# An mLSTM and sparse-attention trunk: nine low parts of weights by ScalarE and an accumulating transfer, with a later low product and other buffer counts

## The chip, the cores and the metric

One core of a Trainium2 chip. The engines are PE (TensorE, matmuls), DVE (VectorE), ACT (ScalarE), POOL (GpSimd) and SP (SyncE, which issues most transfers); 16 DMA engines move data. The metric is the device time of one execution in microseconds (us); lower is better. Before the change the median of 3 runs is 383.62 us (383.25 to 387.83).

## The reference

A decoder trunk of two layers on x of 256 tokens by 1024 channels, in float32. Layer 0 is an mLSTM mixer, layer 1 native sparse attention; each normalises, multiplies by an input weight matrix, mixes, gates, multiplies by an output matrix and adds to x. Cut to the parts that the change touches:

```
x_in, z = jnp.split(h @ w_in, 2, axis=-1)              # h: normalised x; w_in: 1024 x 4096
conv = sum(x_pad[:, tap:tap + S] * conv_w[tap] for tap in range(4))
x_conv = silu(conv + conv_b)
q, k = headwise(x_conv, w_q), headwise(x_conv, w_k)    # 4x4 blocks on the diagonal
v = headwise(x_in, w_v)
gates = concat([q, k, v]) @ w_if + b_if
hh = mlstm_chunkwise(q, k, v, gates)                   # 4 heads of 512
x = x + ((norm(hh) * ln_w + skip * x_conv) * silu(z)) @ w_out
# layer 1: q, compressed / selected / window keys and values, z, gates = rmsnorm(x) @ w_in ...
```

## The kernel before

All large weights are streamed from HBM in 44 units of 1 MB (value units are smaller), in the order of a list `plan`: units 0 to 7 give x_in (two per head), 8 to 15 z, 16 to 23 the output matrix of layer 0, the rest layer 1 (keys and queries, values, z, output). `next_unit` uses unit i and calls `ahead`, so that units up to i+2 have been loaded (`LOOK = 2`).

`load_unit` (L261 to L277) loads a unit in two halves. For each half SP issues a load into a raw buffer `wr` (4 buffers, `WR`), ACT copies it into `wh`, rounded to the matmul format fp32r (L274), and the low part `wl` = raw - wh is a subtraction on POOL if the pair (unit, half) is in the list `ON_POOL`, on DVE otherwise (L275). `wh` and `wl` have 4 buffers each (`WH`). `ON_POOL` holds the second halves (number 1) of units 3 to 10 and 12 to 23, of every other unit from 24 on, and three first halves.

The activations are split in the same way into hh and hl. `project_channels` (L399) multiplies one unit: for 8 slices k and 2 column blocks c three matmuls of 128 columns by 256 tokens each, wh by hh (i = 0), wh by hl (i = 1) and wl by hh (i = 2), 48 in all, at L406. Slices 0 to 3 come from the first half. `LAG` delays the products i = 1 and i = 2 by so many steps of k; unit 1 has its own entry in `LAGS`. `out_project` (L689) and `project_tokens` (L769 to L771) use the other units.

In the first stage, head by head, DVE evacuates x_in with the row scale rb (L433, `xin`; rb is copied at L384, and half of it is made at L385, `rb1h`). `blockdiag` (L390, the multiply at L393) builds on POOL the block-diagonal matrices `m` from a buffer set of 7 (`M2`), two for each of 4 heads. DVE forms products of gate weights (L458, `wtmp`) and sums them into m and q (L459). The convolution is started by ACT (L471, L475) and, in head 0, added up on POOL (L477); DVE adds the other taps (L482), ACT applies silu (L484). PE then makes v from xin and m (L499), q from xc and m (L492, copied by ACT at L493), and the scores from q and xc (L506, L507).

In layer 1 h (L987) is transposed to h1T (L991) and used by PE at L994; `kb` (L811) are keys, half of them written by POOL; L860 are 14 gating multiplications on POOL whose results PE reads at L892.

A scheduler reorders the code: it places every instruction in its engine's queue by a simulated timeline, so that the order on an engine is not that of the code, and a change of one duration or buffer count can move others. Each engine then works through its queue in order.

Of the kernel before, what the change touches and what calls it, by code (L numbers as in the profile page):

```python
# [11 lines left out]
AF = mybir.ActivationFunctionType  # L12
OP = mybir.AluOpType
# [10 lines left out]
G = 4  # L24
NEG = -1e30
F4 = 8
M2 = 7
VA = 2
V_POOL = (0, 2)
SC = 7  # L30
YM = (1,)
LOOK = 2
PSB = {"ps": 2, "pt": 2, "px": 2, "acc0": 1, "acc1": 1}
WH = 4
WR = 4
PB = 5
PV = 4
# [4 lines left out]
VB = 0  # L42
NSW = 1

LAG = (0, 0)
LAGS = {1: (0, 1)}

TR = ((0, 0),)
# [19 lines left out]
NOT_POOL = (0, 1, 2, 11)  # L68
BOTH = (15, 16, 17)
ON_POOL = [(i, 1) for i in list(range(24)) + list(range(24, 48, 2)) if i not in NOT_POOL] + [(i, 0) for i in BOTH]  # L70


_C = {}
# [129 lines left out]
def trunk(ctx, tc, a, out, dbg=None):  # L203
    nc = tc.nc
# [13 lines left out]
    def T(*x, **k):  # L218
        return tile_of(pool[0], *x, **k)

    def TS(*x, **k):
        return tile_of(sb, *x, **k)

    def PS(shape=(P, 512), tag="ps", name="ps"):
        uid[0] += 1
        return pp.tile(list(shape), F32, tag=tag, bufs=PSB[tag], name=f"{name}_{uid[0]}")

    f32 = lambda t: t.bitcast(F32)
    V, A, GP, PE = nc.vector, nc.scalar, nc.gpsimd, nc.tensor
# [11 lines left out]
    def load_x(i):  # L241

        k = slice(2 * i % 4, 2 * i % 4 + 2)
        nc.sync.dma_start(xch0[i // 2][:, k, :].rearrange("p k s -> p (k s)"), a["xt"][:, i * 2 * S:(i + 1) * 2 * S])
# [13 lines left out]
    def load_unit(src, row, nk, nn):  # L258

        hk = nk // 2  # L260
        halves = []  # L261
        for i in range(2):
            raw = TS([P, hk, nn], tag="wr", bufs=WR)
            hi = TS([P, hk, nn], F32R, tag="wh", bufs=WH)
            lo = TS([P, hk, nn], F32R, tag="wl", bufs=WH)
            parts = 1 if loaded else 2
            for j in range(parts):
                if not loaded:
                    load_x(2 * i + j)
                w = hk // parts  # L270
                k = slice(j * w, (j + 1) * w)
                o = i * hk + j * w
                nc.sync.dma_start(raw[:, k, :].rearrange("p k n -> p (k n)"), src[row * P:(row + 1) * P, o * nn:(o + w) * nn])
                A.activation(hi[:, k, :], raw[:, k, :], AF.Copy)  # L274
                (GP if (len(loaded), i) in ON_POOL else V).tensor_tensor(lo[:, k, :], raw[:, k, :], f32(hi[:, k, :]), op=OP.subtract)  # L275
            halves.append((hi, lo))
        return halves  # L277

# [8 lines left out]
    loaded = []  # L287
    used = [0]

    def ahead(n):  # L290
        while len(loaded) < min(n, len(plan)):
            loaded.append(load_unit(*plan[len(loaded)]))
# [98 lines left out]
    def blockdiag(src, dt, n=P):  # L391
        t = T([P, 4, n], dt, tag="m2", bufs=M2)
        GP.tensor_tensor(t[:, :, 0:P].rearrange("p c (n j) -> p c n j", j=4),  # L393
                         src[:, :, None, :].to_broadcast([P, 4, 32, 4]), bm, op=OP.mult)
        return t

    def project_channels(src, row, evac, tag="px"):

        halves = next_unit(src, row, 256)  # L399
        ps = PS((P, 2, S), tag=tag)  # L400
        lags = LAGS.get(used[0] - 1, LAG)

# [23 lines left out]
    for h in range(NH):  # L426
# [61 lines left out]
        for c2 in range(2):  # L488
            ps = PS((P, 2, S))
            for c in range(2):  # L490
                k = 2 * c2 + c
# [88 lines left out]

    oh_ = T([64, 4, P], tag="m2", bufs=M2, name="oh_")
    nc.scalar.dma_start(oh_.rearrange("p h m -> p (h m)"), a["cst"][0:64, n_res:])
    oh = T([64, 4, P], F32R, tag="m2", bufs=M2, name="oh")
    GP.tensor_copy(oh, oh_)
    hns = []
    for h in range(NH):
# [17 lines left out]
        for tb in range(2):  # L604
# [3 lines left out]
            for t in three:  # L608
                jb, o, i, j = t
# [31 lines left out]
    for h in range(NH):  # L641
# [8 lines left out]
        for c2 in range(2):  # L650
# [5 lines left out]
            for c in range(2):  # L656
                k = 2 * c2 + c
# [481 lines left out]
```

## Time and profile before

| | before |
|---|---|
| median of 3 runs | 383.62 us (383.25 to 387.83) |
| profiled execution | 386.84 us, span 385.1 us, mean granted clock 0.959 |
| PE busy | 359.1 us (93%), 2399 instructions |
| DVE busy | 284.8 us (74%), 535 |
| ACT busy | 212.8 us (55%), 405 |
| POOL busy | 192.9 us (50%), 165 |
| chain that ended last | PE 68%, DVE 21%, issue 4%, POOL 3% |
| moved by DMA | 52.74 MB, mean 137 GB/s |

Times within the span count from its start. An engine's busy share over the whole span mixes stages, so the stages are read one by one. A view by waits names, for an idle engine, what ended its idle time; where two engines slow each other there is no wait, and only durations of equal instructions tell it. The granted clock is the share of TensorE's full speed, 2.4 GHz, that was granted; 0.5 is the lower level, 1.2 GHz.

### The profile page before, as it was taken

The numbers are of one execution on the slowest core, as the hardware profiler recorded it, in microseconds if no ns is written. First come the engines' busy times: TensorE is split into PE (matmuls) and PEld (weight loads), VectorE is DVE, ScalarE is ACT, GpSimd is POOL, SyncE is SP. The second block draws the span as 40 slices with busy tenths as digits, with TensorE's granted clock in tenths as the row PEclk, the third lists the DMA queues.
The fourth block names the chain that finished last, engine by engine and source line by source line (L and its number), as shares of the span: only waits on it lengthen the run. The fifth ranks groups of instructions, "written<-read, shape, count | busy, mean of one in ns | idle before, by whom it ended". The sixth has DMA issues, their size and how long they took to land.

```text
span 385.1 us, 6551 instructions
## 1 busy us (share of the span) xinstructions
PE 359.1 (93%) x2399; PEld 319.4 (83%) x2399; DVE 284.8 (74%) x535; ACT 212.8 (55%) x405; POOL 192.9 (50%) x165
## 2 busy tenths in 40 slices
PE   6998797999999999999999999979799989999992
PEld 6997796999999989778888899969799777777761
DVE  5987998678587799996346476799879966685415
ACT  6626284665667564536554542522779648777414
POOL 5238934483324455956345231557434956346303
PEclk9699698999999999999999999989989989999997
DMA  7768323323334311437465962305376331200002
GB/s 260 287 214 299 134 73 108 110 78 143 134 131 154 132 69 45 131 99 252 171 235 199 357 215 75 97 26 155 112 262 217 112 111 55 83 29 2 0 2 109
DMA packets 16880, 52.74 MB, mean 137 GB/s; under 512 B 2000, under 2 KB 2384, under 8 KB 16848
## 3 DMA queue, kind: packets, MB, share of 16 engines
q1 hardware_dynamic: 15472, 48.71, 37.0%
q10 hardware_dynamic: 1376, 3.61, 2.7%
q8 instruction: 19, 0.31, 0.3%
q14 instruction: 13, 0.11, 0.1%
HBM read 50.87 MB, written 1.05 MB: 135 GB/s over the span
## 4 chain that ended last, share of the span: by engine, by line
PE 68%; DVE 21%; issue 4%; POOL 3%; ACT 1%; DMA 1%; POOLq 0%; DVEq 0%
PE ps L406 27%; PE ps L689 16%; DVE xc L482 3%; DVE wl L275 2%; PE ps L506 2%; DVE wtmp L458 2%; PE ps L904 2%; PE ps L892 2%; PE ps L979 2%; PE ps L770 2%; PE ps L769 2%; PE ps L771 2%; DVE r L664 2%; DVE xc L660 1%; PE ps L908 1%
## 5 line engine op out<-in xcount | busy, mean ns | idle before, releaser
L406 PE MATMUL ps<-hT,wh 128*128 128x256 f32 x832 | 163.2, 293 | 0.8 <-ACT wh L274 0.8
L406 PEld LDWEIGHTS ps<-hT,wh 128*128 128x128 f32 x832 | 135.7, 198 | 2.7 <-ACT wh L274 1.1
L275 POOL TENSOR_TENSOR wl<-wr,wh 128x1024 fp32r<-128x1024 f32 (+1 forms) x33 | 85.4, 2593 | 84.9 <-ACT wh L274 72.7
L274 ACT ACTIVATE wh<-wr 128x1024 fp32r<-128x1024 f32 (+2 forms) x90 | 89.3, 1000 | 67.5 <-PE ps L406 27.9
L406 PE MATMUL ps<-hT,wl 128*128 128x256 f32 x416 | 122.1, 294 | 3.5 <-POOL wl L275 1.8
L275 DVE TENSOR_TENSOR wl<-wr,wh 128x1024 fp32r<-128x1024 f32 (+2 forms) x57 | 75.0, 1320 | 29.0 <-ACT wh L274 28.9
L406 PEld LDWEIGHTS ps<-hT,wl 128*128 128x128 f32 x416 | 82.2, 198 | 5.6 <-DVE wl L275 2.2
L689 PE MATMUL ps<-wh,r 128*128 128x512 f32 x128 | 40.9, 399 | 0.5 <-DVE r L664 0.5
L482 DVE SCALAR_TENSOR_TENSOR xc<-xin,pka,xc 128x256 f32<-128x256 f32 x44 | 30.3, 745 | 2.1 <-ACT xc L471 2.1
L689 PEld LDWEIGHTS ps<-wh,r 128*128 128x128 f32 x128 | 23.9, 188 | 6.8 <-DVE r L664 1.4
L689 PE MATMUL ps<-wl,r 128*128 128x512 f32 x64 | 25.0, 396 | 0.0
L689 PE MATMUL ps<-wh,y 128*128 128x512 f32 x64 | 21.9, 405 | 0.0
L770 PE MATMUL ps<-wl,hT 128*128 128x280 f32 (+1 forms) x48 | 16.3, 342 | 1.9 <-DVE wl L275 1.9
L771 PE MATMUL ps<-wh,hT 128*128 128x280 f32 (+1 forms) x48 | 15.8, 339 | 0.0
L769 PE MATMUL ps<-wh,hT 128*128 128x280 f32 (+1 forms) x48 | 15.8, 344 | 0.0
L499 PE MATMUL ps<-m,xin 128*128 128x136 f32 x64 | 10.6, 321 | 5.1 <-DVE m L459 4.4
L798 POOL TENSOR_TENSOR swap<-swap,trig 128x512 f32<-128x512 f32 x6 | 11.0, 1832 | 8.5 <-DMA swap<-kraw 8.5
L689 PEld LDWEIGHTS ps<-wh,y 128*128 128x128 f32 x64 | 11.9, 189 | 3.2 <-issue 0.8
L689 PEld LDWEIGHTS ps<-wl,r 128*128 128x128 f32 x64 | 12.0, 188 | 2.8
L471 ACT ACTIVATE xc<-xin,pka 128x256 f32<-128x256 f32 x16 | 8.9, 592 | 9.8 <-DVE xin L433 9.8
L499 PEld LDWEIGHTS ps<-m,xin 128*128 128x128 f32 x64 | 9.7, 226 | 5.4 <-POOL m L393 5.4
L506 PE MATMUL ps<-q,xc 128*128 128x264 f32 x32 | 11.0, 429 | 2.6 <-ACT q L493 2.6
(472 smaller groups left out, 698.4 us busy)
## 6 DMA issues: line engine op xcount, KB each, us to landing
wr<-in_wi_dram SPq DMA_DIRECT2D x34, 512.0 KB
wr<-in_wo_dram SPq DMA_DIRECT2D x24, 512.0 KB
wr<-in_wi2k_dram SPq DMA_DIRECT2D x12, 512.0 KB
wr<-in_wi2z_dram SPq DMA_DIRECT2D x8, 512.0 KB
wr<-in_wi2v_dram SPq DMA_DIRECT2D x8, 280.0 KB
cw<-in_cw_dram ACTq DMA_DIRECT2D x4, 512.0 KB
xch<-in_xt_dram SPq DMA_DIRECT2D x4, 256.0 KB
wr<-in_wi_dram SPq DMA_DIRECT2D x4, 256.0 KB
```

The source lines that it names most:

```text
L274: A.activation(hi[:, k, :], raw[:, k, :], AF.Copy)
L275: (GP if (len(loaded), i) in ON_POOL else V).tensor_tensor(lo[:, k, :], raw[:, k, :], f32(hi[:, k, :]), op=OP.subtract)
L406: PE.matmul(ps[:, c, :], w, (hl if i == 1 else hh)[:, k, :], start=(k, c, i) == (0, 0, 0), stop=(k, i) == (KT - 1, 2), skip_group_check=True)
L471: A.activation(xc[:, c, :], xin[:, c, 0:S], AF.Identity, scale=tap_w(0, c), bias=cbias)
L482: V.scalar_tensor_tensor(xc[:, c, :], xin[:, c, tap:tap + S], tap_w(tap, c), xc[:, c, :], op0=OP.mult, op1=OP.add)
L499: PE.matmul(ps[:, c, :] if c < 3 else rest[:, tb, :], xin[:, c, 3 + tb * P:3 + (tb + 1) * P], bdv[:, c, :], start=True, stop=True)
L506: PE.matmul(ps[:, 0:SG], xc[:, c, 0:P], q[:, c, :], start=c == 0, stop=False, skip_group_check=True)
L689: PE.matmul(acc, l, r[:, k % 2, cols], start=first and i == 0, stop=last and i == 2)
L769: PE.matmul(o_, lh, hi[:, k % 2, :], start=kt == 0, stop=False)
L770: PE.matmul(o_, lh, lo[:, k % 2, :], start=False, stop=False)
L771: PE.matmul(o_, ll, hi[:, k % 2, :], start=False, stop=kt == KT - 1)
L798: (GP, V)[RE[1]].tensor_tensor(sw, sw, turn(1), op=OP.mult)
```

## The change

For pairs of `ON_POOL` up to unit 12, that is the second halves of units 3 to 10 and 12, nine in all, the subtraction on POOL is replaced: ACT writes -raw, rounded as `wh` is, into `wl`, and POOL issues a transfer from `wr` to `wl`, in SBUF, that adds raw into what stands there. The other 24 POOL subtractions stay. The low product comes four steps of k later in every unit but unit 1 (`LAG`), `wh` and `wl` get 5 buffers, `m` gets 5 instead of 7, and the scratch for descriptors of POOL's transfers is made smaller.

```diff
-M2 = 7
+M2 = 5
-WH = 4
+WH = 5
-LAG = (0, 0)
+LAG = (0, 4)
 LAGS = {1: (0, 1)}
 ON_POOL = [(i, 1) for i in list(range(24)) + list(range(24, 48, 2)) if i not in NOT_POOL] + [(i, 0) for i in BOTH]
+BY_DMA = [(i, j) for i, j in ON_POOL if i <= 12]
                 A.activation(hi[:, k, :], raw[:, k, :], AF.Copy)
-                (GP if (len(loaded), i) in ON_POOL else V).tensor_tensor(lo[:, k, :], raw[:, k, :], f32(hi[:, k, :]), op=OP.subtract)
+                if (len(loaded), i) in BY_DMA:
+
+                    A.activation(lo[:, k, :], raw[:, k, :], AF.Copy, scale=-1.0)
+                    GP.dma_start(out=lo[:, k, :].rearrange("p k n -> p (k n)"), in_=raw[:, k, :].rearrange("p k n -> p (k n)"), accum_op=OP.add)
+                else:
+                    (GP if (len(loaded), i) in ON_POOL else V).tensor_tensor(lo[:, k, :], raw[:, k, :], f32(hi[:, k, :]), op=OP.subtract)
-    nc = _bacc.Bacc("TRN2", target_bir_lowering=False, num_devices=1)
+    nc = _bacc.Bacc("TRN2", target_bir_lowering=False, num_devices=1, dynamic_dma_scratch_size=4096)
```

The scheduler's order changes with it. Three places matter below. (Line numbers of the changed kernel are higher by 7 from L277 on; numbers after names count tiles and differ by a few.)

POOL at the start of the first stage, before: wl_259, wl_396 and wl_458 are the second halves of units 3, 4 and 5, the m are blockdiagonals, xin_578 the clearing of an edge of head 2's xin.

```order
20 L275 TENSOR_TENSOR wl_259<-wr_257,wh_258 128x1024
21 L477 TENSOR_TENSOR xc_324<-xc_324,x_61_325 128x512
22 L393 TENSOR_TENSOR m_57_317<-AT_315,cst_70 128x512
23 L393 TENSOR_TENSOR m_58_319<-pka_71,cst_70 128x4x128
...
27 L393 TENSOR_TENSOR m_117_706<-pka_71,cst_70 128x4x128
28 L393 TENSOR_TENSOR m_145_896<-AT_315,cst_70 128x512
29 L477 TENSOR_TENSOR xc_324<-xc_324,x_61_325 128x512
30 L275 TENSOR_TENSOR wl_396<-wr_394,wh_395 128x1024
31 L275 TENSOR_TENSOR wl_458<-wr_456,wh_457 128x1024
34 L428 MEMSET xin_578 128x4x3
```

And with the change:

```order
20 L280 DMA wl_259<-wr_257 128x1024
21 L484 TENSOR_TENSOR xc_325<-xc_325,x_61_326 128x512
22 L400 TENSOR_TENSOR m_57_318<-AT_316,cst_70 128x512
23 L400 TENSOR_TENSOR m_58_320<-pka_71,cst_70 128x4x128
...
26 L400 TENSOR_TENSOR m_116_709<-AT_316,cst_70 128x512
27 L484 TENSOR_TENSOR xc_325<-xc_325,x_61_326 128x512
28 L280 DMA wl_397<-wr_395 128x1024
29 L400 TENSOR_TENSOR m_117_711<-pka_71,cst_70 128x4x128
30 L435 MEMSET xin_581 128x4x3
31 L280 DMA wl_460<-wr_458 128x1024
```

Five blockdiagonals instead of seven stand together, the subtractions have become transfers, and the third transfer stands behind m_117 and the memset of xin_581.

DVE in the same stage, from the first convolution steps to the sum that fills head 0's second blockdiagonal (m2_58), before:

```order
33 L482 SCALAR_TENSOR_TENSOR xc_60_324<-xin_33_159,pka_7_71,xc_60_324 128x256 x2
34 L458 TENSOR_TENSOR wtmp_59_321<-wif_47_242,pka_7_71 128x128
35 L458 TENSOR_TENSOR wtmp_63_346<-wif_46_241,pka_7_71 128x256
36 L482 SCALAR_TENSOR_TENSOR xc_60_324<-xin_33_159,pka_7_71,xc_60_324 128x256 x2
37 L459 TENSOR_REDUCE m2_58_319<-wtmp_59_321 128x4x8
38 L459 TENSOR_REDUCE q_62_345<-wtmp_63_346 128x4x8
```

And with the change:

```order
33 L489 SCALAR_TENSOR_TENSOR xc_60_325<-xin_33_159,pka_7_71,xc_60_325 128x256 x4
34 L465 TENSOR_TENSOR wtmp_59_322<-wif_47_242,pka_7_71 128x128
35 L465 TENSOR_TENSOR wtmp_63_347<-wif_46_241,pka_7_71 128x256
36 L466 TENSOR_REDUCE m2_58_320<-wtmp_59_322 128x4x8
37 L466 TENSOR_REDUCE q_62_346<-wtmp_63_347 128x4x8
```

The same seven instructions stand ahead of the sums. On PE, 14 more matmuls (10 of L406, 4 of L499) stand ahead of the first score matmul L506; on DVE in layer 1 kb no longer stands between h (L987) and h1T (L991).

POOL in layer 1, before: wl_3112 is the second half of the third z unit of layer 1, the p are gatings.

```order
100 L798 TENSOR_TENSOR swap_2188<-swap_2188,trig_2186 128x512
101 L860 TENSOR_SCALAR p__486_2821<-p__486_2821,sums_2816,gt_2192 128x128
...
108 L860 TENSOR_SCALAR p__508_2885<-p__508_2885,sums_2853,gt_2192 128x256 x2
109 L275 TENSOR_TENSOR wl_3112<-wr_3110,wh_3111 128x1024
110 L860 TENSOR_SCALAR p__560_3173<-p__560_3173,sums_3168,gt_2192 128x128
```

And with the change:

```order
99 L282 TENSOR_TENSOR wl_2987<-wr_2985,wh_2986 128x1024
100 L282 TENSOR_TENSOR wl_3121<-wr_3119,wh_3120 128x1024
101 L867 TENSOR_SCALAR p__486_2830<-p__486_2830,sums_2825,gt_2201 128x128
102 L867 TENSOR_SCALAR p__489_2839<-p__489_2839,sums_2825,gt_2201 128x256 x2
```

The subtraction has moved from behind the gatings to ahead of them.

## Rows read from the trace of the kernel before

**Rows 1.** Windows: length, busy us (instructions) of PE, PEld, DVE, ACT, POOL; clock, DMA share, GB/s.

```profile
36.00:63.00 27.00, 19.31 (x130) 18.52 (x129) 26.76 (x39) 12.30 (x20) 17.79 (x14) 0.87 0.37 131
86.00:130.00 44.00, 44.00 (x346) 42.52 (x346) 31.85 (x49) 27.63 (x41) 16.99 (x9) 1.00 0.41 144
...
40.00:50.00 10.00, 8.27 (x46) 8.12 (x47) 10.00 (x13) 4.21 (x8) 8.60 (x5) 0.67 0.44 156
```

**Rows 2.** Timeline of PE: start, us, operation, count, idle time before and its releaser.

```profile
41.03 3.97 PE L499 MATMUL ps<-m,xin 128*128 128x136 f32 x16 [4.40 <-DVE m L459]
...
62.66 0.71 PE L506 MATMUL ps<-q,xc 128*128 128x264 f32 x2 [2.60 <-ACT q L493]
...
254.97 0.69 PE L994 MATMUL ps<-h1T,pkb 128*128 128x64 f32 x2 [2.70 <-DVE h1T L991]
...
309.27 0.46 PE L406 MATMUL ps<-hT,wl 128*128 128x256 f32 x1 [1.78 <-POOL wl L275]
```

**Rows 3.** Chain that ended last, in order of time: start, us, what.

```profile
31.09 0.04 DVE wl L275
...
59.76 1.28 DVE xc L482 x3
...
109.34 11.38 PE ps L406 x95
```

**Rows 4.** Timeline of ACT.

```profile
20.64 1.06 ACT L274 ACTIVATE wh<-wr 128x1024 fp32r<-128x1024 f32 x1 [1.88 <-DMA wr<-in_wi_dram]
...
40.16 1.06 ACT L274 ACTIVATE wh<-wr 128x1024 fp32r<-128x1024 f32 x1 [5.42 <-DMA wr<-in_wi_dram]
...
61.06 1.06 ACT L484 ACTIVATE xc<-xc 128x1024 f32<-128x1024 f32 x1 [3.45 <-DVE xc L482]
```

**Rows 5.** Timeline of DVE.

```profile
23.60 0.42 DVE L384 COPY rb<-ps 128x256 f32<-128x256 f32 x1 [1.72 <-PE ps L373]
...
25.08 2.50 DVE L385 TENSOR_SCALAR rb1h<-rb 128x256 f32<-128x256 f32 x1
...
33.54 2.45 DVE L482 SCALAR_TENSOR_TENSOR xc<-xin,pka,xc 128x256 f32<-128x256 f32 x2
35.91 2.31 DVE L458 TENSOR_TENSOR wtmp<-wif,pka 128x128 f32<-128x128 f32 x2
...
42.73 4.96 DVE L458 TENSOR_TENSOR wtmp<-wif,pka 128x128 f32<-128x128 f32 x2
...
49.02 0.61 DVE L458 TENSOR_TENSOR wtmp<-wif,pka 128x128 f32<-128x128 f32 x2
...
50.65 0.87 DVE L482 SCALAR_TENSOR_TENSOR xc<-xin,pka,xc 128x256 f32<-128x256 f32 x2
...
251.31 3.29 DVE L811 TENSOR_TENSOR kb<-rot,ka 64x1024 fp32r<-64x1024 f32 x1
```

**Rows 6.** Timeline of POOL (the first of its seven blockdiagonals, L393, among them).

```profile
24.05 3.37 POOL L275 TENSOR_TENSOR wl<-wr,wh 128x1024 fp32r<-128x1024 f32 x1 [4.96 <-ACT wh L274]
...
31.43 2.04 POOL L393 TENSOR_TENSOR m<-AT,cst 128x512 f32<-128x512 f32 x1
...
41.69 5.72 POOL L275 TENSOR_TENSOR wl<-wr,wh 128x1024 fp32r<-128x1024 f32 x2
...
306.87 2.34 POOL L275 TENSOR_TENSOR wl<-wr,wh 128x1024 fp32r<-128x1024 f32 x1
```

**Rows 7.** Instructions grouped by line and shape: busy us, mean ns, idle time before.

```profile
L275 POOL TENSOR_TENSOR wl<-wr,wh 128x1024 fp32r<-128x1024 f32 x31 | 82.5, 2666 | 74.3 <-ACT wh L274 62.1 <-PE ps L970 9.2 <-issue 1.8
L274 ACT ACTIVATE wh<-wr 128x1024 fp32r<-128x1024 f32 x78 | 81.7, 1054 | 55.3 <-PE ps L406 21.1 <-PE ps L689 14.9 <-DMA wr<-in_wi_dram 8.6
```

**Rows 8.** Timeline of SP's queue: issues of loads, 512 KB each, and their count.

```profile
16.20 9.31 SPq L273 DMA_DIRECT2D wr<-in_wi_dram  x5
...
30.63 0.47 SPq L273 DMA_DIRECT2D wr<-in_wi_dram  x1
```

**Rows 9.** Windows of line L406 alone: length, PE and PEld busy (instructions), clock, DMA share, GB/s.

```profile
63.00:130.00 67.00, 47.36 (x356) 44.18 (x356) 0.97 0.36 126
```

## The prediction

> **What bounds the kernel now.** I read the windows first, to see where TensorE is not full. From 86 to 130 us PE is busy in all 44.00 us; in 36:63 it is busy 19.31 of 27.00 us, while DVE is busy 26.76 of 27.00 and POOL 17.79 [rows 1]. So the one long stretch in which PE starves is 36 to 63 us: 27.00 - 19.31 = 7.69 us idle, and in addition a granted clock of 0.67 in 40:50, where part of the work ran at the lower level, 1.2 GHz [rows 1].
>
> PE's timeline, then, says for whom it waits. In this stretch it stood 4.40 us before 41.03 for DVE's blockdiagonal m and 2.60 us before 62.66 for ACT's q; two later waits are of the same size, 2.70 us for h1T and 1.78 us for a POOL low part [rows 2]. The chain of waits has nothing but DVE and its issue gaps from 31.09 to 61.04 us [rows 3]. In ACT's timeline q comes right behind the silu at 61.06, for which ACT had waited 3.45 us on the convolution, DVE's [rows 4].
>
> Why DVE is so slow there is in the timelines of DVE and POOL side by side. The same pair of wtmp products takes 0.61 us at 49.02, when POOL is idle, 4.96 us at 42.73 and 2.31 us at 35.91 [rows 5]; POOL runs two wl subtractions from 41.69 for 5.72 us, and its seven blockdiagonals from 31.43 on, 1.1 to 2.0 us each, to about 40.3 [rows 6]. Two convolution steps take 0.87 us at 50.65 and 2.45 us at 33.54. The copy rb1h takes 2.50 us at 25.08, inside the wl of 24.05 to 27.42 [rows 5, 6]. So in this stretch DVE bounds PE, and POOL's subtractions and blockdiagonals make DVE slow.
>
> **The change, part by part.**
>
> *Nine POOL subtractions removed.* At 2666 ns each [rows 7] that is 24.0 us of POOL between 24 and 130 us; what counts is what DVE did beside them on the chain. (a) wl_259 beside rb1h: rb1h read one 128x256 tensor, as the copy ahead of it, which took 0.42 us [rows 5]: 2.50 - 0.42 = 2.1 us earlier xin, for which ACT's convolution copies wait. (b) wl_396 and wl_458 beside wtmp: 4.96 - 0.61 = 4.35 us. The other six lie where PE is full [rows 1] and give nothing.
>
> *M2 from 7 to 5.* Two of seven blockdiagonals leave the run of POOL work at 31.43 to 40.3 us and come later, one by one. The excess of DVE there is (2.45 - 0.87) x 2 + (2.31 - 0.61) = 4.86 us, the second pair of convolution steps, at 38.15, having the same 2.45 us; two sevenths of it are 1.4 us. Sum on DVE's chain: 2.1 + 4.35 + 1.4 = 7.85 us.
>
> Not all of this reaches PE. The stretch from 49 to 61 us, convolutions beside no subtraction, keeps its price, and q still stands behind the silu; fourteen more matmuls stand ahead of q's consumers, which fill 14 x 0.12 = 1.7 us of the wait (0.12 us is the spacing where PE is full: 11.38 us for 95 matmuls in the chain [rows 3]). I take 6 us. Upper bound: all idle time, 7.69, with the clock that comes back, about 9 (the clock's 1.3 is an estimate: 0.33 x 10 us in 40:50 less some 2 us in which PE was idle there [rows 1]). Lower bound 1, if new neighbours on DVE (below) take it.
>
> *Nine ACT copies added.* 1054 ns each, as hi [rows 7]: 9.5 us. ACT is busy 12.30 of 27.00 in 36:63 and has idle time before its copies [rows 1, 4]: 0. Without that cover three of them, ahead of 45 us, would cost 3.2 us.
>
> *Nine accumulating transfers added.* No row shows one. Nearest rows: a plain load of the same 512 KB, issued at 16.20 and read at 20.64, so 20.64 - 16.20 = 4.4 us; one behind about 2 MB of other loads, issued at 30.63 and read at 40.16, 9.5 us [rows 4, 8]. From below, nothing excludes 2.67, the POOL subtraction itself [rows 7]. I take 5 us, near the first, since the DMA engines are busy 0.37 of 36:63 [rows 1]. By the Trainium skill ("DMA: Bandwidth & Descriptors", "Anatomy of one DMA — SWDGE (gpsimd) path") a transfer issued by GpSimd takes about 2.0 us plus its bytes at 436 GB/s, an estimate of 3.2 us here, and the term below would be 0; no run so far shows it.
>
> *LAG (0,4)* pays for that: the second half's low part is now needed eight matmuls before a unit's end, 40 instead of 26 matmuls into it, 40 x 0.12 = 4.8 us after its start; hi of the second half is needed at 16 instead of 24, 1 us earlier, covered by a lookahead of two units. The tight place is wl_460: on POOL its transfer stands behind blockdiagonal m_117 (which needs a buffer PE frees) and behind the xin memset, that is behind DVE's last convolution of head 0, which I put at about 45 us; landing 50, needed by PE at about 50. Price 1 us, bounds 0 and 9.5 - 4.4 = 5.1, rounded to 6 with the clock.
>
> *WH 4 to 5* costs nothing in time; the descriptor scratch neither.
>
> *Later places, only moved.* (c) DVE at 251.31 spends 3.29 us on kb, ahead of h1T, for which PE waits 2.70 us [rows 2, 5, 6]; now kb is no longer between h and h1T. Take 2; bounds 4.2 (with the lower clock after it) and -1, if the new order makes another wait. (d) POOL's wl at 306.87, behind fourteen gatings, held PE for 1.78 us until 309.27 [rows 2, 6]; now that wl is taken ahead of the gatings. Take 2 with the clock; bounds 3.9 and -2, as the gatings move by 2.34 us and PE's L892 uses them.
>
> **Sum.** 6 + 2 + 2 - 1 = 9 us. Against the profiled execution: 386.84 - 9 = 377.8. That execution lies 3.2 us above the median of 383.62, so on the median 374.6 (2.3% less).
>
> **Rivals.**
>
> *The gain is absorbed.* For it: DVE was busy 26.76 of 27.00 us; the blockdiagonals that remain still run beside the convolutions, and two come later, beside others; ACT waits 3.45 us for the silu's input whatever POOL does. Then only 1 to 4 us of (a) and (b) reach PE, (c) and (d) cancel with new waits: 380 to 384. Against it: 4.35 us of DVE's chain goes at one place that PE demonstrably waited for.
>
> *Slower: transfers land so late that raw buffers run out.* A raw buffer was free once the subtraction had read it; now it is held until the transfer has landed. There are four, two units' worth. In 63:130 PE does 356 weight matmuls, 7.4 units in 67 us, 9.0 us a unit [rows 9], so a buffer may be held 18.1 us: load 4.4, hi 1.05, negated copy 1.05, landing L. It breaks even at L = 11.6 us. Beyond that each two units lose L - 11.6; at 15 us that is 3.4 x 3.7 = 12.6 us, 377.8 + 12.6 - 3.2 = 387.2; slower by over 2% (391.3) from L = 16. For it: DMA 9.5 us under load [rows 4, 8], and nothing shows what an add costs the DMA engines. Against: a share of 0.41 in 86:130 leaves them more than half idle [rows 1].
>
> *Transfers wait for DVE.* POOL and DVE hold each other up in rows 5 and 6; if preparing a transfer does so too, in 36:63 (DVE busy 99%) each waits for a gap. With one group of 2.5 us for each of wl_397 and wl_460, PE waits up to 5 us, the sum is 4, 379.6 on the median; in 86:130 DVE has 12 us free of 44 [rows 1] and nothing is lost. The Trainium skill states such a rule ("SBUF — State Buffer", "SBUF: two separate sides"): GpSimd cannot write descriptors while VectorE holds the port pair they share, and the transfer only seems slow. The mutual slowing in rows 5 and 6 agrees with a shared port; no run yet shows a transfer.
>
> *The change doesn't do what it says*: hardly possible, the order lists nine transfers in place of nine subtractions.
>
> **How the numbers follow.** Forecast (366 to 379) 0.58; absorbed 0.18; waiting for DVE 0.12; landings of 16 us or more, with any stall at a place not foreseen that costs as much, 0.12. The predicted time is 374.6. The range 366 to 388 reaches down to the largest sum of bounds (9 + 4.2 + 3.9 = 17.1 us of gain, 366.5) and up to landings of 15 us (387.2); it leaves out the last case. A measurement can tell about 2% here: below 375.9 is faster, above 391.3 slower. Of the forecast 0.45 lies below 375.9, since there is more room below the sum than above it; its other 0.13 and the first two rivals lie within 2%; the last case is slower.
>
> **What would show it.** Right: wtmp pairs at about 0.6 us and rb1h at 0.4; PE's wait for m under 1.5 us and for q smaller; PE busy above 24 of 27 us in the stretch; waits for h1T and for POOL's wl gone; no wait for a transfer's wl above 1 us. Wrong: PE or SP waiting for transfers, landings above 10 us, DVE steps still 1.2 us each, or L499 and L506 waits of the old size with another releaser.

## The result: 1.5% slower

The changed kernel takes 389.79 us (median of 4 runs, 389.31 to 391.61) against 384.38 us for the kernel before beside it (383.25 to 387.83): a ratio of 1.0149, 95% interval 1.0103 to 1.0196. The forecast was 374.6 us; the time lies above the range of 366 to 388, on the other side of no change. The profiled execution has a span of 387.5 us at a mean granted clock of 0.979, so the clock is not what was lost.

The windows of the changed kernel, with the columns of [rows 1], then two windows of before:

```profile
36.00:63.00 27.00, 24.08 (x171) 23.15 (x170) 27.00 (x46) 18.89 (x28) 15.72 (x16) 0.94 0.71 199
63.00:86.00 23.00, 20.25 (x145) 18.84 (x144) 15.83 (x20) 14.21 (x26) 10.97 (x8) 1.00 0.61 159
...
110.00:130.00 20.00, 17.45 (x124) 15.59 (x124) 16.90 (x21) 12.80 (x20) 8.13 (x4) 1.00 0.60 176
130.00:166.00 36.00, 31.22 (x210) 28.21 (x209) 35.41 (x76) 19.46 (x27) 21.51 (x18) 0.96 0.20 67
```

```profile
63.00:86.00 23.00, 23.00 (x149) 21.47 (x148) 16.01 (x21) 14.06 (x26) 14.98 (x9) 0.93 0.27 94
...
130.00:166.00 36.00, 35.58 (x235) 31.35 (x233) 34.72 (x72) 20.10 (x29) 25.29 (x20) 1.00 0.25 88
```

From 36 to 63 us PE is busy 24.08 us where it was 19.31 [rows 1]: the gain that was forecast is there. From 63 us on PE is idle where it had been full or nearly so: 2.75 us of 63:86, 2.55 of 110:130 and 4.78 of 130:166, in which DVE is busy 35.41 of 36.00. The waits of PE in the changed kernel say for whom (waiting line and releaser, us in total, times, longest):

```profile
PE ps L848 <- DVE nm L854: 4.2, 1, 4.2
PE ps L506 <- DVE m L466: 2.6, 1, 2.6
PE ps L499 <- DVE gsc L518: 2.4, 1, 2.4
PE ps L661 <- ACT hn L641: 2.3, 1, 2.3
PE ps L661 <- DVE xc L665: 1.7, 1, 1.7
...
PE ps L413 <- DMA wl<-wr: 1.1, 1, 1.1
```

The waits for h1T and for POOL's low part [rows 2] are gone, the wait for m has shrunk from 4.4 to 2.6 us, and new ones stand in their place: q's (L499), the normalised heads hn (L661) and the first scores of layer 1 (L848). In DVE's timeline the two prices on which the forecast rested have fallen as it said, rb1h from 2.50 to 0.29 us and the wtmp pair of 42.73 from 4.96 to 0.61 [rows 5]; what runs beside the five blockdiagonals is as slow as before:

```profile
23.97 0.29 DVE L392 TENSOR_SCALAR rb1h<-rb 128x256 f32<-128x256 f32 x1
...
31.61 4.83 DVE L489 SCALAR_TENSOR_TENSOR xc<-xin,pka,xc 128x256 f32<-128x256 f32 x4
36.37 2.53 DVE L465 TENSOR_TENSOR wtmp<-wif,pka 128x128 f32<-128x128 f32 x2
...
40.76 0.61 DVE L465 TENSOR_TENSOR wtmp<-wif,pka 128x128 f32<-128x128 f32 x2
```

POOL's timeline, before and changed, around the last head's small operations (t is a power, s = r t, nb = nb t; ACT needs s and nb to write hn of head 3):

```profile
149.89 0.20 POOL L630 TENSOR_TENSOR s<-r,t 128x2 f32<-128x2 f32 x1
...
150.46 5.76 POOL L275 TENSOR_TENSOR wl<-wr,wh 128x1024 fp32r<-128x1024 f32 x2 [0.23 <-ACT wh L274]
```

```profile
150.14 5.64 POOL L282 TENSOR_TENSOR wl<-wr,wh 128x1024 fp32r<-128x1024 f32 x2 [2.48 <-PE ps L413]
155.88 0.69 POOL L635 TENSOR_TENSOR t<-t,mhalf 128x2 f32<-128x2 f32 x1
156.66 3.32 POOL L667 TENSOR_TENSOR xc<-xc,z 128x1024 f32<-128x1024 f32 x1
159.94 1.25 POOL L637 TENSOR_TENSOR s<-r,t 128x2 f32<-128x2 f32 x1
```

Before, s came ahead of the pair of subtractions, at 149.89; now it stands behind the pair and behind a gating of y (L667), at 159.94. These are the low parts of units 16 and 17, whose code the change does not touch: the scheduler moved them.

To see where the kernels part, the table gives the end of the 480th weight matmul (unit 9), the first of the four transposes that start the gates' chain, and the first and last matmul of the output projections, all in us from one profiled execution each, with the ratio to the kernel before from all runs. "Lag" is the later low product; "wh/wl" and "m" are the buffer counts.

| kernel | unit 9 ends | gates start | first output | last output | ratio (95%) |
|---|---|---|---|---|---|
| before | 107.5 | 108.7 | 158.7 | 377.7 | 1 |
| changed: transfers, lag, 5 wh/wl, 5 m | 103.0 | 105.8 | 162.4 | 379.9 | 1.0149 (1.0103 to 1.0196) |
| tail_first: changed, one order on POOL | 104.9 | 107.7 | 160.1 | 377.5 | 0.9973 (0.9938 to 1.0008) |
| no_transfer: lag, 5 wh/wl, 5 m | 112.2 | 113.6 | 170.1 | 385.7 | 1.0214 (1.0165 to 1.0263) |
| transfers_and_lag: 4 wh/wl, 7 m | 101.2 | 101.2 | 154.0 | 370.3 | 0.9804 (0.9748 to 0.9860) |
| transfers_only: 4 wh/wl, 7 m | 103.3 | 105.3 | 154.7 | 375.7 | 0.9898 (0.9855 to 0.9940) |
| lag_only: 4 wh/wl, 7 m | 109.5 | 110.9 | 166.8 | 383.3 | 1.0162 (1.0106 to 1.0219) |
| m2_7: transfers, lag, 5 wh/wl, 7 m | 102.6 | 102.9 | 157.3 | 375.1 | 0.9939 (0.9896 to 0.9982) |
| m2_7_tail: m2_7, one order on POOL | 102.2 | 102.5 | 152.9 | 370.1 | 0.9825 (0.9767 to 0.9883) |
| wh_4: transfers, lag, 4 wh/wl, 5 m | 101.9 | 104.7 | 163.7 | 380.0 | 1.0192 (1.0115 to 1.0268) |
| wh_4_tail: wh_4, one order on POOL | 102.6 | 105.4 | 154.7 | 373.1 | 0.9954 (0.9912 to 0.9996) |
| three_transfers: lag, 4 wh/wl, 7 m | 108.7 | 110.1 | 164.7 | 380.9 | 1.0176 (1.0095 to 1.0257) |
| nm_first: m2_7_tail, one order on DVE | 101.6 | 101.9 | 152.3 | 367.3 | 0.9845 (0.9779 to 0.9911) |

The changed kernel is 4.5 us ahead at unit 9, 2.9 us ahead where the gates start, and 3.8 us behind at the first output matmul. So 8.3 us went between 103 and 162 us. Ratios are the comparison to trust: the kernel before itself had medians of 384.38 to 387.48 us beside these runs, and the end of unit 0, ahead of the first transfer, scatters from 15.6 to 18.4 us over these traces. A stretch between two points of one trace is safer than a single point.

### The profile page after: what moved, and what is told of

Its sections match the earlier page's. It is cut to its first block, busy times and chain, and to the rows that moved or that the text cites. A ratio compares the mean times of both kernels' runs of the same rounds, so it can differ in the third digit from the quotient of the medians.

```text
span 387.5 us, 6559 instructions
## 1 busy us (share of the span) xinstructions
PE 355.2 (92%) x2399; PEld 315.4 (81%) x2399; DVE 283.0 (73%) x535; ACT 221.4 (57%) x414; POOL 175.7 (45%) x165
## 4 chain that ended last, share of the span: by engine, by line
PE 54%; DVE 26%; issue 7%; DMA 5%; ACT 4%; POOL 1%; SPq 1%; POOLq 0%; DVEq 0%; ACTq 0%
PE ps L696 17%; PE ps L413 16%; DVE xc L489 6%; DVE wl L282 4%; PE ps L911 2%; PE ps L899 2%; PE ps L848 2%; PE ps L986 2%; DMA cst<-in_cst_dram 2%; PE ps L849 1%; PE ps L778 1%; DVE w L608 1%; ACT wh L276 1%; DMA wr<-in_wi_dram 1%; PE ps L777 1%
## 5 line engine op out<-in xcount | busy, mean ns | idle before, releaser
L413 PE MATMUL ps<-hT,wh 128*128 128x256 f32 x832 | 139.1, 292 | 2.8 <-DVE hT L345 1.5
L413 PEld LDWEIGHTS ps<-hT,wh 128*128 128x128 f32 x832 | 120.9, 197 | 6.5 <-DVE hT L345 2.0
L282 DVE TENSOR_TENSOR wl<-wr,wh 128x1024 fp32r<-128x1024 f32 (+2 forms) x57 | 77.4, 1359 | 27.2 <-ACT wh L276 22.3
L413 PE MATMUL ps<-hT,wl 128*128 128x256 f32 x416 | 87.8, 285 | 1.1 <-DMA wl<-wr 1.1
L282 POOL TENSOR_TENSOR wl<-wr,wh 128x1024 fp32r<-128x1024 f32 (+1 forms) x24 | 60.3, 2518 | 58.5 <-ACT wh L276 29.0
L413 PEld LDWEIGHTS ps<-hT,wl 128*128 128x128 f32 x416 | 66.3, 192 | 2.3 <-issue 1.9
L280 POOL DMA_DIRECT2D wl<-wr x9 | 8.1, 898 | 23.6 <-ACT wl L279 22.9
L848 PE MATMUL ps<-ka,qt 128*128 128x256 f32 (+1 forms) x32 | 12.9, 407 | 4.2 <-DVE nm L854 4.2
L643 POOL TENSOR_TENSOR xc<-xc,pka 128x1024 f32<-128x1024 f32 x4 | 9.8, 2452 | 12.2 <-PE ps L514 12.2
L696 PE MATMUL ps<-wl,y 128*128 128x512 f32 x32 | 12.7, 398 | 0.0
```

The source lines that it names most:

```text
L280: GP.dma_start(out=lo[:, k, :].rearrange("p k n -> p (k n)"), in_=raw[:, k, :].rearrange("p k n -> p (k n)"), accum_op=OP.add)
L413: PE.matmul(ps[:, c, :], w, (hl if i == 1 else hh)[:, k, :], start=(k, c, i) == (0, 0, 0), stop=(k, i) == (KT - 1, 2), skip_group_check=True)
L643: GP.tensor_tensor(xcs[h], xcs[h], CA("skip")[:, 4 * h:4 * h + 4, None].to_broadcast([P, 4, S]), op=OP.mult)
L696: PE.matmul(acc, l, r[:, k % 2, cols], start=first and i == 0, stop=last and i == 2)
L848: PE.matmul(o_, lq, ka[:, g, :, 0:w_], start=True, stop=False)
```

## The experiments

**One place of POOL's order.** The theory after the traces: engines work through their queues in order, and the tail of head 3 (its small operations t, s and nb) behind two subtractions is what PE waits for at L661. The rivals: DVE sets the pace there whatever POOL does; or the transfers themselves cost. tail_first adds ordering edges, which fix who comes first in a queue, and nothing else (cut to what acts; YM is head 1):

```diff
+                elif (len(loaded), i) in [(16, 1), (17, 0)]:
+                    with tc.issue_after(tail[3].ins):      # tail[3]: nb of head 3
+                        GP.tensor_tensor(lo[:, k, :], raw[:, k, :], f32(hi[:, k, :]), op=OP.subtract)
...
+        if h in YM:
+            with tc.issue_after(tail[3].ins):
+                GP.tensor_tensor(y, y, z, op=OP.mult)
```

> The changed kernel with one place of POOL's order altered: two subtractions (units 16 and 17) and the gating of head 1's y now stand behind the three small operations of head 3 (s, nb) instead of ahead of them. Theory, order: in the changed kernel PE's two waits for hn and xc before L661 (2.3 and 1.7 us) come from those three small operations standing behind 9 us of POOL work; here hn of head 3 comes at about 151 us instead of 161, both waits fall below 1 us in sum, the first L689 comes at 158 to 159.5 us (162.4 in the changed kernel), and the time falls by 2.5 to 4 us, to 386 to 387.5. Rival, DVE: DVE is busy 35.41 of 36 us there and sets the pace whatever POOL's order is; the time stays within 1 us of 389.8. Rival, transfers: nothing here touches them; no change.

385.63 us, ratio 0.9973 against the changed kernel's 1.0149, and both waits at L661 are absent from its list of waits. The first output matmul came at 160.1, not 158 to 159.5, since this execution was 1.9 us later at unit 9 already. From there to the first output it takes 55.2 us, the changed kernel 59.4. The order theory holds for this place, and DVE as the sole pace-maker falls.

**The transfers taken away.**

```diff
-BY_DMA = [(i, j) for i, j in ON_POOL if i <= 12]
+BY_DMA = []
```

> The changed kernel with all nine subtractions back on POOL; later low product, 5 wh/wl and 5 blockdiagonal buffers stay. POOL's order around head 3 is as in the changed kernel (its small operations behind two subtractions). Theory, order: the first stage loses the gain of 4.5 us (unit 9 ends at 106 us or later, 102.97 in the changed kernel), the loss between 110 and 162 us stays, at least 4 us of it, and the time is 390 to 394. Rival, transfers: if the transfers are what costs (raw buffers held until landing, SP waiting 34 us for them), the time falls to 386 or less.

394.92 us, ratio 1.0214, just above what was expected and slower than the changed kernel, so the transfers are not its loss. Unit 9 ends 9.2 us later than with them. Its longest waits of PE are those of the first stage:

```profile
PE ps L499 <- ACT xc L491: 4.8, 1, 4.8
PE ps L506 <- DVE m L466: 4.6, 1, 4.6
```

**Transfers and lag without the buffer counts; transfers alone.**

From the changed kernel, transfers_and_lag takes back the two counts:

```diff
-WH = 5
+WH = 4
-M2 = 5
+M2 = 7
```

> The changed kernel with 4 wh/wl buffers and 7 blockdiagonal buffers as before: transfers and the later low product alone. Here the scheduler places head 3's small operations on POOL ahead of the subtractions of units 16 and 17. Theory, order: unit 9 ends near 103 us, no wait above 1 us for hn at L661, and the time is 380 to 385. Rival, transfers or the lag: as slow as the changed kernel, 388 to 391. Rival, blockdiagonals: with seven of them in a row again DVE's first stage is 1 to 2 us slower, 103 becomes 105.

379.38 us, ratio 0.9804, faster than the kernel before by 1.4 to 2.5%. No wait for hn of head 3 (1.1 us for another operand at L661); PE is full from 63 to 130 us.

transfers_only takes back the lag as well:

```diff
-LAG = (0, 4)
+LAG = (0, 0)
```

> The kernel before with the nine transfers alone (no lag, 4 wh/wl buffers, 7 blockdiagonal buffers). A transfer landed 5.8 us after its issue in the changed kernel, and without the lag the second half's low part is needed 26 instead of 40 matmuls into a unit, 1.7 us earlier. Theory, order: PE's waits for transferred wl grow from 1.1 us to 3 to 6 us, part of the first stage's gain is lost (unit 9 ends at 104 to 107 us); head 3's small operations stand ahead here, so the loss behind 110 us is small: 382 to 387. Rival, transfers: the time stays at 389 or above.

381.92 us, ratio 0.9898. PE waited 0.6 us for transferred low parts, not 3 to 6: that expectation was wrong, the transfers come in time without the lag too. What PE waits for more is m and xin in the first stage. With transfers, the lag is worth about 1%; the two intervals just touch.

**The lag alone, on the kernel before.**

```diff
-LAG = (0, 0)
+LAG = (0, 4)
```

> The kernel before with the later low product alone (nine subtractions on POOL, 4 wh/wl and 7 blockdiagonal buffers). POOL's subtractions slow DVE in the first stage as before, so theory (the transfers give the gain there) expects unit 9 to end at 106 to 109 us (107.47 before, 101.24 with transfers and lag), wtmp beside two subtractions again near 5 us, and a time within 2% of before, 381 to 388. Rival (the lag gives the gain): unit 9 ends near 102 us and the time is 377 to 381.

392.29 us, ratio 1.0162: slower than the kernel before, and above the 381 to 388 us that were expected. The gain of the first stage is indeed not the lag's (unit 9 ends at 109.5). PE waits 3.6 us for the silu's output in the first stage, the gates start 2.1 us later, and the first output matmul comes 8.2 us later. Of these 8.2 us 6.2 lie between the end of unit 9 and that matmul: PE waits 2.2 us for DVE's z, and behind that wait the granted clock is 0.50, the lower level, in 125:130, where the kernel before has 1.00. Why the lag puts DVE's z late I did not settle.

```profile
PE ps L492 <- ACT xc L484: 3.6, 1, 3.6
...
PE ps L406 <- DVE z L647: 2.2, 1, 2.2
```

**Blockdiagonal buffers against wh/wl buffers, with and without the tail.** m2_7 is the changed kernel with `M2 = 7`, wh_4 with `WH = 4`; m2_7_tail and wh_4_tail add the ordering edges of tail_first.

> The changed kernel with 7 instead of 5 blockdiagonal buffers; 5 wh/wl buffers stay. Head 3's small operations stand behind two subtractions on POOL as in the changed kernel. Theory, two costs: with seven buffers the blockdiagonals m of heads 2 and 3 no longer stand ahead of transfers on POOL, unit 9 ends at 101 to 102 us (102.97 in the changed kernel, 101.24 with transfers and lag); the tail still costs 3 to 4 us at L661; first L689 at 157 to 160, time 382 to 386. Rival (the blockdiagonals cost nothing, all comes from the tail): 388 to 390 as the changed kernel.

383.44 us, ratio 0.9939, first output matmul at 157.3, as the theory of two costs had it.

> The changed kernel with 4 instead of 5 wh and wl buffers; 5 blockdiagonal buffers stay. Head 3's small operations (s, nb) stand on POOL behind four subtractions and a gating, further back than in the changed kernel. Theory, order: unit 9 ends near 103 us; hn of head 3 comes at 160 us or later, PE waits 4 us or more at L661, and the time is 387 to 392. Rival (the fifth buffer pair costs): 380 to 384.

392.13 us, ratio 1.0192, at the upper end of what was expected, and one wait of PE stands out:

```profile
PE ps L661 <- ACT hn L641: 9.2, 1, 9.2
```

Here s and nb of head 3 stood behind four subtractions, and POOL reached s only at 161.18:

```profile
155.57 5.64 POOL L282 TENSOR_TENSOR wl<-wr,wh 128x1024 fp32r<-128x1024 f32 x2
161.18 1.17 POOL L637 TENSOR_TENSOR s<-r,t 128x2 f32<-128x2 f32 x1
```

> The changed kernel with 7 blockdiagonal buffers and head 3's small operations on POOL ahead of the two subtractions: both suspected costs taken away, 5 wh/wl buffers kept. Theory, two costs: like transfers and lag alone, 377 to 381, first L689 at 154 to 156 us. Rival (the fifth wh/wl buffers cost): 384 or above.

378.93 us, ratio 0.9825, first output matmul at 152.9.

> The changed kernel with 4 instead of 5 wh/wl buffers (5 blockdiagonal buffers) and head 3's small operations ahead of the subtraction of unit 16 second half and the gating. Without the tail edit PE waited 9.2 us for hn at L661 and the time was 392.1. Theory (the tail's place on POOL is that wait; the fifth pair of wh/wl buffers is worth little by itself): the wait falls below 2 us, and the time to 384 to 387, as the changed kernel with the tail edit (385.6). Rival (fewer buffers cost): 388 or more.

382.79 us, ratio 0.9954, faster than the 384 to 387 us expected, and the wait of 9.2 us is gone.

The eight kernels with nine transfers and the lag thus lay out the causes. The tail's place: 1.0149 to 0.9973, 0.9939 to 0.9825 and 1.0192 to 0.9954, that is 1.1 to 2.4%. Five instead of seven blockdiagonal buffers, tail in place: 0.9825 to 0.9973 with five wh/wl buffers, 0.9804 to 0.9954 with four, 1.5% each time. Four or five wh/wl buffers, tail in place: 0.9954 and 0.9973, 0.9804 and 0.9825, nothing beyond the intervals.

The fifth pair of wh/wl buffers does cost where it moves the tail. From transfers_and_lag (0.9804) that edit alone gives m2_7 (0.9939), since with it the scheduler puts head 3's operations behind the two subtractions; from there the edit of M2 alone gives the changed kernel (1.0149). The stretch from the end of unit 9 to the first output shows that these two are the whole loss of that stretch. PE is busy 51 to 52 us in it in each of these traces, and takes 51.2 us in the kernel before, 59.4 in the changed kernel, 55.2 with the tail in place, 54.8 with seven blockdiagonal buffers, and 50.7 with both (m2_7_tail), where PE is never idle in 130:166:

```profile
130.00:166.00 36.00, 36.00 (x236) 32.32 (x235) 34.22 (x63) 19.05 (x25) 24.05 (x17) 1.00 0.27 83
```

**Three transfers instead of nine**, on the kernel transfers_and_lag:

```diff
-BY_DMA = [(i, j) for i, j in ON_POOL if i <= 12]
+BY_DMA = [(i, j) for i, j in ON_POOL if i <= 5]
```

> Transfers and lag (4 wh/wl, 7 blockdiagonal buffers), but only the first three of the nine low parts (units 3, 4, 5) by transfer; the other six are subtracted on POOL again. By the prediction's step these six lie where PE is full and give nothing: 378 to 381 as with nine, unit 9 ends near 101 us. Rival (they slow DVE's gate chain, which PE waits for behind 110 us): unit 9 as before, the transposes of the gates 2 us later or more, 382 to 386.

390.67 us, ratio 1.0176 against 0.9804 with nine, slower than either expectation: the six later ones are worth 3.7%, and the step that gave them nothing is wrong. The first three do give their gain in three_transfers: unit 5 ends at 55.5 us, with the lag and no transfer (lag_only) at 64.1. But by unit 9 it is gone (108.7 and 109.5), and so it is in the ratios (1.0176 and 1.0162). In 63:86 PE is busy 17.97 us of 23.00, in transfers_and_lag all 23.00; its waits there stand at q's matmuls, for DVE:

```profile
PE ps L499 <- DVE gsc L518: 5.0, 2, 3.0
```

The groups by line and shape (busy us, mean ns of one) show the convolution on DVE, 44 equal instructions, in three_transfers, in transfers_and_lag and in the changed kernel:

```profile
L489 DVE SCALAR_TENSOR_TENSOR xc<-xin,pka,xc 128x256 f32<-128x256 f32 x44 | 36.4, 882 | 1.3 <-ACT xc L478 1.3
```

```profile
L489 DVE SCALAR_TENSOR_TENSOR xc<-xin,pka,xc 128x256 f32<-128x256 f32 x44 | 25.5, 631 | 2.8 <-ACT xc L478 2.8
```

```profile
L489 DVE SCALAR_TENSOR_TENSOR xc<-xin,pka,xc 128x256 f32<-128x256 f32 x44 | 31.1, 760 | 0.1
```

The same work differs by 10.9 us with what POOL does beside it: in all 13 traces, a step beside which POOL ran no instruction took 0.46 to 0.49 us, and every step above 0.6 us lay beside a POOL instruction. The place in three_transfers, four convolution steps of head 3 in 6.27 us beside three POOL operations in a row (DVE, then POOL):

```profile
76.94 6.27 DVE L489 SCALAR_TENSOR_TENSOR xc<-xin,pka,xc 128x256 f32<-128x256 f32 x4 [0.73 <-ACT xc L478]
```

```profile
75.62 2.37 POOL L282 TENSOR_TENSOR wl<-wr,wh 128x1024 fp32r<-128x1024 f32 x1 [2.19 <-ACT q L500]
77.95 2.08 POOL L643 TENSOR_TENSOR xc<-xc,pka 128x1024 f32<-128x1024 f32 x1
79.99 2.55 POOL L536 TENSOR_TENSOR vsp<-v,vsp 128x1024 fp32r<-128x1024 f32 x1
```

and six steps of the same head in transfers_and_lag, while a transfer that POOL had issued at 71.83 was under way:

```profile
72.05 2.56 DVE L489 SCALAR_TENSOR_TENSOR xc<-xin,pka,xc 128x256 f32<-128x256 f32 x6 [1.38 <-ACT xc L478]
```

The chain that ended last goes through DVE's convolutions from 61 to 70 us and from 77 to 83 us in three_transfers; in transfers_and_lag it is PE alone there.

**One place of DVE's order**, on m2_7_tail: in layer 1 a rotation sum and a low part stood ahead of the first nm of the scores, 2.37 and 2.42 us in DVE's timeline of m2_7_tail, and PE waited 4.2 us.

```profile
267.64 2.37 DVE L815 TENSOR_TENSOR rot<-rot,swap 128x512 f32<-128x512 f32 x1 [0.59 <-POOL swap L814]
269.93 2.42 DVE L286 TENSOR_TENSOR wl<-wr,wh 128x560 fp32r<-128x560 f32 x1
272.28 0.28 DVE L863 CUSTOM_DVE_ANT_0 p__486_2830<-ps,cst 128x128 f32<-128x128 f32 x1
```

nm_first puts both behind the fourth nm, with ordering edges as above (the low part is that of unit 35, first half).

> The changed kernel with 7 blockdiagonal buffers, head 3's small operations on POOL ahead of two subtractions, and one more place altered, on DVE in layer 1: the first four steps nm of the scores stand ahead of a rotation sum and a low part instead of behind them. PE waited 4.2 us for nm there (line of the score matmuls ka, qt). Theory (the order on in-order engines is what costs): that wait falls to 1 us or less, and the time to 375 to 377.5 (378.9 without this edit). Rival (PE is given back at the next stop, DVE's scores run on as before): 378 to 380.

378.0 us, ratio 0.9845. The wait fell to 2.4 us in two pieces, 1.9 the longest, and in the profiled execution the last output matmul came 2.8 us earlier, but the ratio is not told apart from m2_7_tail's 0.9825. Inconclusive for the time.

```profile
PE ps L861 <- DVE nm L867: 2.4, 2, 1.9
```

The fastest versions are transfers_and_lag, m2_7_tail and nm_first; among the three the intervals do not choose. transfers_and_lag needs no ordering edges.

## Why the prediction was wrong, step by step

**What bounds the kernel: right for its stretch, wrong as a whole.** In 24 to 63 us DVE bounds PE and POOL slows DVE: rb1h and the wtmp pair fell to about an eighth once the subtractions beside them went. But I read PE's full windows from 63 to 130 us as a stage bound by PE, and DVE's share of 31.85 in 44.00 as room. PE was full there in the order of the kernel before. Beside it runs the chain of gates and heads on DVE, ACT and POOL, and where the new order delays that chain, PE runs out of work. The chain does not shorten the gain by itself: in m2_7_tail PE is busy all 36.00 us of 130:166 with DVE busy 34.22, and what was won by unit 9 is still there at the first output.

**The steps that failed: the two buffer counts, and the order that came with them.** The transfers and the lag alone gave 2.0% (0.9804) where 2.3% was forecast for the whole change. The fifth wh/wl pair, put at nothing, and five blockdiagonal buffers, put at a gain of 1.4 us, then cost 3.5% together (0.9804 to 0.9939 to 1.0149), some 13 us. That 2.0% comes so near is in part luck, since the six transfers counted at nothing are in it.

**(a), (b), the term of 6 us: right in mechanism, smaller in the changed kernel.** Unit 9 ended 4.5 us earlier there, but 1.5 of these are there at the end of unit 0, ahead of any transfer. From the end of unit 0 to that of unit 9 the changed kernel gained 3.0 us, transfers_and_lag 7.0, the six later transfers included. Of the signs named, PE's 24 us of 27 came, but its wait for m fell to 2.6 us and not under 1.5, one for q of 2.4 us has DVE as its releaser, and the first four convolution steps still take 1.2 us each.

**"The other six lie where PE is full and give nothing": wrong.** Nine transfers against three: 0.9804 against 1.0176. The six subtractions slow DVE's convolutions from 60 us on, and PE, full there in the kernel before, waits for q behind them once it is early.

**M2, a gain of 1.4 us: wrong in sign.** It costs 1.5%, about 6 us, with the tail in place. There was no gain where it was sought: four convolution steps and a wtmp pair beside the five blockdiagonals take 4.83 and 2.53 us, before 2 x 2.45 and 2.31 [rows 5]. With five buffers POOL stands still until PE's v has freed one:

```profile
42.56 1.04 POOL L400 TENSOR_TENSOR m<-pka,cst 128x512 f32<-128x512 f32 x1 [3.12 <-PE ps L506]
...
50.64 1.32 POOL L400 TENSOR_TENSOR m<-AT,cst 128x512 f32<-128x512 f32 x1 [1.79 <-PE ps L506]
```

The last blockdiagonal starts at 57.17 us, with seven buffers (m2_7) at 44.00. The gates start 2.95 us later (105.81 against 102.86) though PE's unit 9 ends within 0.4 us: 505 weight matmuls instead of 484 stand ahead of them in PE's order. That the late blockdiagonals are why the scheduler puts head 3 there is likely, but not shown.

**ACT copies at nothing: right; wh/wl buffers at nothing: right only with the tail in place.** No new wait of PE in the first stages is for those copies. With the tail in place wh 4 or 5 made no difference; with seven blockdiagonal buffers the fifth pair cost 1.4% by moving the tail. The scratch size was not tried alone.

**Transfers, 5 us to land, price 1 us: right in size, at another place.** They landed in 4.5, 5.8 and 8.9 us (least, median, most), and PE waited 1.1 us for one, the first, not for wl_460; in three_transfers that first wait was 3.1 us. The view of the tile wl on POOL, changed kernel, has them in one line:

```profile
DMA to landing us min/median/max: 4.5/5.8/8.9
```

The estimate of 3.2 us from the Trainium skill ("DMA: Bandwidth & Descriptors", "Anatomy of one DMA — SWDGE (gpsimd) path") is too short here by 2.6 us; the measurement decides.

**LAG: the reason given was wrong.** It was to pay for the landing, but without it PE waited only 0.6 us for transferred low parts. It is worth about 1% with the transfers, where PE waits less for m and xin with it, and costs 1.6% without them.

**(c), (d), 4 us: both waits went, as said, and less than half was gained.** In the moved order the scores' wait of 4.2 us at L848 came in their place; every run with five wh/wl buffers has it (until nm_first's edit), none with four. From the first to the last output matmul, a stretch that holds all three, the changed kernel takes 217.5 us against 219.1: 1.6 us.

**The rivals.** Late landing did not come: SP waited 34.2 us for landings, 7.8 at most, but PE starved of no weights. Waiting for DVE did not come as a price: the four transfers that POOL issued in 36:63, where DVE was busy all 27.00 us, landed in 4.5 to 5.8 us; the one of 8.9 us, issued at 24.87, was ahead of that. "Absorbed" had the gain lost, but at another place, and had no term for a loss beyond it. The step that is missing in the prediction is the one for work the diff does not touch, which cost 1.8% here (tail_first): I followed the order at the three places where a wait stood before, and did not read POOL's queue around the next stage, where a comparison of the orders shows s behind two subtractions ahead of any run.

## What to carry to other kernels

When a stall goes, look for the chain that comes next and ask whether the kernel has the order for it: on queues worked in order, a tiny operation behind two large ones that nobody needs yet can cost more than the stall did. Where a scheduler places the work, read the whole order of the engines that feed the next bound, and pin the small operations of the chain ahead of bulk work. Try a change of buffer counts apart from the mechanism that it comes with. And an engine off the path is not free: count what its neighbours' instructions cost beside it before giving it work "where PE is full".

## What the runs showed of the hardware

How much DVE pays for POOL's neighbourhood was more than expected: 44 equal convolution steps took 25.5 to 36.4 us, 631 to 882 ns each, and the whole excess lies at steps beside POOL instructions. In three_transfers a step that began at 62.18 us, beside a subtraction from 62.02 to 64.39, took 2.49 us. An accumulating transfer of 512 KB, issued by POOL, holds POOL for 0.88 us instead of 2.67 [rows 7] and showed no such effect on DVE: six steps in 2.56 us while one was under way, and 0.47 to 0.49 us for each of the 45 steps of the traces that had nothing of POOL beside them but such an issue. The Trainium skill ("SBUF — State Buffer", "SBUF: two separate sides") says that of the engines VectorE and GpSimd alone share a port pair, held for a whole instruction; both observations agree with it. Its warning that transfers issued by GpSimd starve while VectorE runs an instruction in a two-port mode is not shown by these runs: 5.8 us was the longest landing of those issued in 36:63, in which DVE had no idle time, and no trace tells which of DVE's instructions run in such a mode.
